# Four column tiles for the modulations that TensorE computes during the S5 scan

## The chip, the cores and the metric

The kernel runs on one core of a Trainium2 chip. The metric is the device time of one execution in microseconds; the kernel before takes 2045.85 us in the median of three runs (2044.94 to 2045.88).

## The reference

Two transformer-like blocks run one after the other on 256 tokens of width 1024, all in 32-bit floats. The first has attention and a mixture of 32 experts. The second has two layers, a retention layer and an S5 layer (a diagonal state-space scan), each followed by a convolutional feed-forward part. Every layer of the second block is modulated by a condition vector:

```
cond = silu(c)                                  # 1024 numbers
mod  = cond @ ada_w[i] + ada_b[i]               # 1024 x 6144 weights, for i = 0, 1
sh1, sc1, g1, sh2, sc2, g2 = split(mod, 6)
h = rms_norm(x) * (1 + sc1) + sh1
x = x + g1 * mixer(h)                           # retention for i = 0, S5 for i = 1
h = rms_norm(x) * (1 + sc2) + sh2
x = x + g2 * conv_ffn(h)
```

So there are twelve groups of 1024 modulations, each a product of one row of 1024 numbers with a 1024 x 1024 matrix (4 MB). The change concerns one of them, `sc2` of the S5 layer.

## The kernel before

A feature of the width-1024 vectors stands on a partition, so modulations are wanted as columns: 128 partitions by 8 columns for a group. Class `Columns` makes them. For eleven of the twelve groups `step` (L192) does it on VectorE: for each chunk `k` of 128 input features it multiplies the weights of that chunk (128 x 1024) by the chunk's condition number per partition and adds them up in `acc` (L201, L203), and `finish` (L208) sums over the partitions with eight matmuls against a column of ones (L214).

The group that `ADA_PE` names, number 10 (`sc2` of the S5 layer), is done by `part` (L220) on TensorE instead, during the scan. Its weights lie in memory as eight pieces of 128 x 1024: four for output features 0 to 511 and four for 512 to 1023, each with two chunks `k` of 512 columns. One call of `part` takes one piece and does two matmuls. The stationary operand is one column, `cond[:, k]`, and the moving one is 128 x 512 weights, so that the result is one row of 512 on one partition, added up over eight chunks in a bank of the accumulators (tile `s`). Behind every fourth call ScalarE copies the row out (L233), four transposes turn it into four columns (L236), and VectorE adds the bias (L239) and one (L241) into `mod`.

The pieces come through the stream `wa2`, a ring of two buffers of 128 x 1024 (`NADA2 = 2`). A load into a buffer is issued when the instruction that read the piece before last is done. These loads go through GpSimd's queue (POOL, L115), in order with the loads of the scan's own matrices (tiles `s5i` and `s5e`, L1779).

The scan has eight chunks `c`. `rotated_inputs(c)` makes its inputs with 16 matmul records (L1790), `scan(c)` runs on VectorE (L1801 to L1814), and `from_states(c)` gives the outputs with 8 records on L1825 and 16 on L1827. Chunks go in pairs to `gelu` (L1835 to L1840, ScalarE and VectorE in turn). `outputs` puts the result back in the order of tokens (L1757). Then come the gated products of the layer (`glu_half`, L251 to L253), which start behind `from_states(7)`. The loop calls `fill` twice for each chunk, and the table `FILL` says how many parts are to have been traced by then:

```
for c in range(8):
    if c < 7:
        rotated_inputs(c + 1)
    scan(c)
    fill(2 * c)
    ...
    last = from_states(c)
    fill(2 * c + 1)
```

The order on each engine is not that of the program: a planner with a cost model of its own goes through the program by priority and places an instruction where its engine is free by its reckoning. On the chip each engine then follows that fixed order, and an instruction that waits holds up all behind it. Behind the scan, `ada_step(4)` starts the next group on VectorE at low priority.

The same kernel uses column tiles at its start: `ada_tile` (L405) makes the first block's modulations with stationary operands of 32 columns (one or two of them in use, the rest zero) and puts the outputs of four matmuls on partitions 0 to 31, 32 to 63, 64 to 95 and 96 to 127 of one bank.

Of the kernel before, what the change touches and what calls it, by code (L numbers as in the profile page):

```python
# [8 lines left out]
F32 = mybir.dt.float32  # L9
# [20 lines left out]
ADA_PE = (10,)  # L30

ADA_F1 = (4, 7, 10, 13)
FILL = (0, 0, 0, 0, 1, 2, 3, 4, 5, 6, 7, 8, 8, 8, 8, 8, 8)
PREP_RET = 4
AHEAD = 2
LOW = 300
# [29 lines left out]
class Stream:  # L66
# [3 lines left out]
    def __init__(self, nc, pool, n, width, late=None):  # L70
        self.nc, self.pool, self.n, self.width, self.late = nc, pool, n, width, late
        self.sources, self.tiles, self.home = [], {}, {}
        self.issued = self.at = 0
        self.held = {}
# [109 lines left out]
class Columns:  # L184
# [2 lines left out]

    def __init__(self, g, cond, out, bias, scales):
        self.g, self.cond, self.out, self.bias, self.scales = g, cond, out, bias, scales
        self.n, self.u, self.pool, self.acc = 0, 3, None, None  # L190

    def step(self, bank=None):  # L192

# [25 lines left out]

    def part(self, bank, pool):  # L220

        g = self.g
        v = g.nc.vector
        u = self.u = (self.u + 1) % 4
        if u == 0:
            self.b = bank()
        w = g.wa.get()
        for k in range(2 * u, 2 * u + 2):
            g.nc.tensor.matmul(out=self.b[:1, :], lhsT=self.cond[:, k:k + 1], rhs=w[:, k % 2 * 512:(k % 2 + 1) * 512], start=(k == 0), stop=(k == 7))
        g.wa.issue(g.wa.at)  # L230
        if u == 3:
            row = pool.tile([1, 512], F32, tag="row", name="row")
            g.nc.scalar.copy(out=row, in_=self.b[:1, :])  # L233
            b = bank()
            for m in range(4):
                g.nc.tensor.transpose(out=b[:, m:m + 1], in_=row[:, m * 128:(m + 1) * 128], identity=g.ident[:1, :1])  # L236
            sl = slice(2 * self.n, 2 * self.n + 4)
            o = self.out[:, sl]
            v.tensor_tensor(out=o, in0=b[:, :4], in1=self.bias[:, sl], op=ALU.add)  # L239
            if self.n // 4 in self.scales:  # L240
                v.tensor_scalar(out=o, in0=o, scalar1=1.0, scalar2=None, op0=ALU.add)  # L241
            self.n += 2
# [1005 lines left out]
def sincos(nc, part, ang, n, out=None):  # L1248

    v, s = nc.vector, nc.scalar  # L1250
    k, r, m = part(n), part(n), part(n)
    v.tensor_scalar(out=k, in0=ang, scalar1=INV2PI, scalar2=MAGIC, op0=ALU.mult, op1=ALU.add)
    v.tensor_scalar(out=k, in0=k, scalar1=-MAGIC, scalar2=None, op0=ALU.add)
    v.scalar_tensor_tensor(out=r, in0=k, scalar=-TWOPI[0], in1=ang, op0=ALU.mult, op1=ALU.add)
    v.scalar_tensor_tensor(out=r, in0=k, scalar=-TWOPI[1], in1=r, op0=ALU.mult, op1=ALU.add)
    v.scalar_tensor_tensor(out=r, in0=k, scalar=-TWOPI[2], in1=r, op0=ALU.mult, op1=ALU.add)

    v.tensor_scalar(out=m, in0=r, scalar1=HALFPI, scalar2=-2 * HALFPI * 2, op0=ALU.is_gt, op1=ALU.mult)
    v.scalar_tensor_tensor(out=m, in0=r, scalar=HALFPI, in1=m, op0=ALU.add, op1=ALU.add)
    for t in (r, m):  # L1260
        v.tensor_scalar(out=t, in0=t, scalar1=PI_IN, scalar2=-PI_IN, op0=ALU.min, op1=ALU.max)
    c, sn = out or (part(n), part(n))
    s.activation(out=sn, in_=r, func=ACTF.Sin)
    s.activation(out=c, in_=m, func=ACTF.Sin)
    return c, sn
# [195 lines left out]
def second_block(tc, g, out):  # L1461
# [261 lines left out]
    with ExitStack() as e5:  # L1723
# [132 lines left out]
        def fill(i):  # L1856
            while at[0] < FILL[i]:
                ada.part(small_bank, p5)
                at[0] += 1
# [303 lines left out]
```

## Time and profile before

| what | value |
|---|---|
| median of 3 runs | 2045.85 us |
| the profiled execution: its time | 2045.55 us |
| the profiled execution: its span | 2043.9 us |
| TensorE matmul busy | 1943.4 us (95%) |
| VectorE busy | 1104.8 us (54%) |
| ScalarE busy | 649.2 us (32%) |
| GpSimd busy | 59.0 us (3%) |

The shares are means over the whole span. The stretch of the scan, 1700 to 1784 us, is a small part of it with limits of its own. A 32-bit matmul leaves two records in the trace, so a group of "x8" is four matmuls of the program. The time of an execution is 1.65 us longer than its span.

### The profile page before, as it was taken

What the parts mean: (1) busy time and instruction counts of PE and PEld (TensorE: products, weight loads), DVE (VectorE), ACT (ScalarE), POOL (GpSimd) and SP (SyncE); (2) the same over time, 40 slices, a digit from 0 to 9 for tenths busy, and PEclk for the clock granted to TensorE, in tenths of its full rate; (3) what the DMA queues carried; (4) which work ended last, traced back from release to release, by engine and by line L of the source; (5) the groups of instructions that cost most, each with busy time, mean ns of one, the idle gap of its engine ahead of it and who ended that gap; (6) DMA issues with size and microseconds to landing.
All of it is one profiled execution on the core that took longest, in us unless ns stands there. A gap on an engine that the chain in (4) does not pass through costs nothing. (4 is left out here: it accounts for less than half of the span.)

```text
span 2043.9 us, 29004 instructions
## 1 busy us (share of the span) xinstructions
PE 1943.4 (95%) x11188; PEld 1256.4 (61%) x11188; DVE 1104.8 (54%) x2360; ACT 649.2 (32%) x1134; POOL 59.0 (3%) x92
## 2 busy tenths in 40 slices
PE   6999989999999999999989999999999999999998
PEld 4756844333233333343333338888999998699998
DVE  3856654322222122132212238998898879779863
ACT  5455211000000000010000014445677645256542
POOL 1000010000000000000000000000011002100000
PEclk9999989999999999999999998999999999799999
DMA  8657659999999999999989994767677877555651
GB/s 342 223 197 282 240 193 413 427 426 427 426 427 427 426 427 427 426 421 387 427 366 427 426 394 159 259 235 267 228 258 260 288 279 295 206 193 195 226 178 63
DMA packets 101758, 643.41 MB, mean 315 GB/s; under 512 B 11584, under 2 KB 12880, under 8 KB 34288
## 3 DMA queue, kind: packets, MB, share of 16 engines
q1 hardware_dynamic: 94176, 613.46, 75.8%
q0 software_dynamic: 6624, 26.76, 3.8%
q8 instruction: 89, 1.46, 0.3%
q10 hardware_dynamic: 816, 1.30, 0.2%
q14 instruction: 53, 0.43, 0.1%
HBM read 626.79 MB, written 14.68 MB: 314 GB/s over the span
## 5 line engine op out<-in xcount | busy, mean ns | idle before, releaser
L956 PE MATMUL hc<-w,xe 128*64 128x512 f32 (+1 forms) x2008 | 470.3, 596 | 29.5 <-DMA w<-in_w_in_dram 28.3
L956 PEld LDWEIGHTS hc<-w,xe 128*64 128x64 f32 (+1 forms) x2008 | 145.4, 138 | 338.7 <-issue 244.0
L148 DVE TENSOR_TENSOR parts<-w,parts 128x1024 fp32r<-128x1024 f32 x238 | 289.8, 1222 | 64.2 <-ACT parts L147 60.0
L147 ACT CAST parts<-w 128x1024 fp32r<-128x1024 f32 x238 | 248.6, 1047 | 200.3 <-PE b L253 116.5
L251 PE MATMUL b<-h2h,parts 128*128 128x256 f32 x896 | 255.9, 286 | 1.4 <-ACT h2h L1527 0.9
L252 PE MATMUL b<-h2l,parts 128*128 128x256 f32 x896 | 255.5, 285 | 1.3 <-DVE h2l L1528 0.9
L956 PE MATMUL yb<-w,hb 128*64 128x512 f32 (+1 forms) x1024 | 252.5, 603 | 2.1 <-SPq L1205 1.6
L253 PE MATMUL b<-h2h,parts 128*128 128x256 f32 x896 | 254.3, 284 | 0.0
L976 DVE COPY hs<-hc 128x512 f32<-128x512 f32 x33 | 22.8, 691 | 405.3 <-PE hc L956 405.3
L251 PEld LDWEIGHTS b<-h2h,parts 128*128 128x128 f32 x896 | 170.1, 190 | 4.0 <-ACT h2h L1527 3.0
L252 PEld LDWEIGHTS b<-h2l,parts 128*128 128x128 f32 x896 | 169.9, 190 | 3.7 <-DVE h2l L1528 2.1
L253 PEld LDWEIGHTS b<-h2h,parts 128*128 128x128 f32 x896 | 169.8, 190 | 0.6 <-issue 0.6
L974 ACT COPY hs<-hc 128x512 f32<-128x512 f32 x33 | 19.3, 585 | 429.9 <-PE hc L956 429.9
L956 PEld LDWEIGHTS yb<-w,hb 128*64 128x64 f32 (+1 forms) x1024 | 68.1, 138 | 132.1 <-issue 120.9
L203 DVE SCALAR_TENSOR_TENSOR acc<-w,c,acc 128x1024 f32<-128x1024 f32 x77 | 98.5, 1279 | 7.3 <-DMA w<-in_ada_w_dram 7.0
L251 PE MATMUL b<-ah,parts 128*128 128x256 f32 x352 | 101.3, 288 | 0.7 <-ACT parts L147 0.6
L253 PE MATMUL b<-ah,parts 128*128 128x256 f32 x352 | 101.2, 287 | 0.0
L252 PE MATMUL b<-al,parts 128*128 128x256 f32 x352 | 100.5, 286 | 0.0
L938 PEld LDWEIGHTS gb<-S,h 128*128 128x128 f32 x544 | 68.2, 202 | 40.6 <-issue 30.9
L1019 ACT COPY ys<-yb 64x512 f32<-64x512 f32 (+1 forms) x32 | 18.5, 578 | 222.6 <-PE yb L956 222.5
L1562 PE MATMUL b<-parts,h2h 128*128 128x512 f32 x256 | 81.9, 400 | 1.4 <-DVE parts L148 0.8
L938 PE MATMUL gb<-S,h 128*128 128x128 f32 (+1 forms) x544 | 76.1, 293 | 6.2 <-issue 5.0
(521 smaller groups left out, 2967.0 us busy)
## 6 DMA issues: line engine op xcount, KB each, us to landing
w<-in_w_in_dram SPq DMA_DIRECT2D x252, 1024.0 KB, 19.4
w<-in_w_out_dram SPq DMA_DIRECT2D x128, 1024.0 KB, 19.5
w<-in_ffn_up_dram SPq DMA_DIRECT2D x44, 1024.0 KB, 4.9
w<-in_ada_w_dram SPq DMA_DIRECT2D x72, 512.0 KB, 5.1
w<-in_ret_w_in_dram SPq DMA_DIRECT2D x24, 1024.0 KB, 4.8
w<-in_ffn_down_dram SPq DMA_DIRECT2D x22, 1024.0 KB, 4.9
w<-in_w_ada_dram SPq DMA_DIRECT2D x32, 512.0 KB, 3.9
w<-in_ada_w_dram POOLq DMA_DIRECT2D x24, 512.0 KB, 4.8
```

Of the source, the lines that this page charges most:

```text
L147: self.nc.scalar.copy(out=hi, in_=w)
L148: self.nc.vector.tensor_tensor(out=lo, in0=w, in1=hi.bitcast(F32), op=ALU.subtract)
L203: v.scalar_tensor_tensor(out=self.acc, in0=w, scalar=cc, in1=self.acc, op0=ALU.mult, op1=ALU.add)
L251: pe.matmul(out=o, lhsT=w[0][:, sl], rhs=a[0][:, k], start=first, stop=False)
L252: pe.matmul(out=o, lhsT=w[0][:, sl], rhs=a[1][:, k], start=False, stop=False)
L253: pe.matmul(out=o, lhsT=w[1][:, sl], rhs=a[0][:, k], start=False, stop=last)
L938: g.got = pe.matmul(out=b[:, k * 128:k * 128 + n], lhsT=g.h2[:, t, d * 128:(d + 1) * 128], rhs=S[:, t, :n], start=(t == 0), stop=(t == 1))
L956: g.got = pe.matmul(out=on, lhsT=x, rhs=w[:, n * 512:n * 512 + 512], start=first, stop=last)
L974: s.copy(out=h, in_=hc[e][n])
L976: v.tensor_copy(out=h, in_=hc[e][n])
L1019: s.copy(out=o, in_=i)
L1562: pe.matmul(out=bs[t], lhsT=x[:, kk, tsl], rhs=y[:, k * 512:(k + 1) * 512], start=(kk == 0 and i == 0), stop=(kk == 7 and i == 2))
```

## The change

One call of `part` now takes two pieces (four chunks `k`) and does four matmuls. The condition is copied once into `padded`, 128 x 8 x 32, which GpSimd zeroes, so that each chunk has a stationary operand of 32 columns with the number in column 0. The four matmuls of a call write to the four column tiles of the bank (partitions 0, 32, 64 and 96 in use), and the second call adds to the first: two calls make 512 features where four calls did. ScalarE copies the whole bank, 128 x 512. In place of four transposes of one row, four matmuls against a column of ones both turn the row and sum it over the partitions. `FILL` counts to four calls instead of eight and puts them at every other place: behind `from_states` of chunks 2, 3, 4 and 5.

```
-FILL = (0, 0, 0, 0, 1, 2, 3, 4, 5, 6, 7, 8, 8, 8, 8, 8, 8)
+FILL = (0, 0, 0, 0, 0, 1, 1, 2, 2, 3, 3, 4, 4, 4, 4, 4, 4)
...
-        u = self.u = (self.u + 1) % 4
+        u = self.u = (self.u + 1) % 2
         if u == 0:
             self.b = bank()
-        w = g.wa.get()
-        for k in range(2 * u, 2 * u + 2):
-            g.nc.tensor.matmul(out=self.b[:1, :], lhsT=self.cond[:, k:k + 1], rhs=w[:, k % 2 * 512:(k % 2 + 1) * 512], start=(k == 0), stop=(k == 7))
+        if self.padded is None:
+            self.padded = pool.tile([128, 8, 32], F32, name="padded")
+            g.nc.gpsimd.memset(self.padded, 0.0)
+            v.tensor_copy(out=self.padded[:, :, 0], in_=self.cond)
+        ws = [g.wa.get() for _ in range(2)]
+        for k in range(4):
+            g.nc.tensor.matmul(out=self.b[32 * k:32 * k + 32, :], lhsT=self.padded[:, 4 * u + k], rhs=ws[k // 2][:, k % 2 * 512:(k % 2 + 1) * 512],
+                               start=(u == 0), stop=(u == 1))
         g.wa.issue(g.wa.at)
-        if u == 3:
-            row = pool.tile([1, 512], F32, tag="row", name="row")
-            g.nc.scalar.copy(out=row, in_=self.b[:1, :])
+        if u == 1:
+            row = pool.tile([128, 512], F32, tag="row", name="row")
+            g.nc.scalar.copy(out=row, in_=self.b)
             b = bank()
             for m in range(4):
-                g.nc.tensor.transpose(out=b[:, m:m + 1], in_=row[:, m * 128:(m + 1) * 128], identity=g.ident[:1, :1])
+                g.nc.tensor.matmul(out=b[:, m:m + 1], lhsT=row[:, m * 128:(m + 1) * 128], rhs=g.ones[:, :1], start=True, stop=True)
```

## Rows read from the trace of the kernel before

**Rows 1.** L229's records: nanoseconds min/median/max, first and last start, forms.
```profile
L229 PE MATMUL s<-w,c x32: 590/592/1057, 1701.0 to 1771.7; 128*1 128x512 f32 x32
```

**Rows 2.** Timeline: start, length, L405's and L229's groups on TensorE.
```profile
15.41 1.93 PE L405 MATMUL pm<-w,cz 128*32 128x512 f32 x8 [15.41 <-DVE rst L179]
...
19.95 1.07 PE L405 MATMUL pm<-w,cz 128*32 128x512 f32 x8
20.95 0.71 PE L412 MATMUL b<-dg,xr 128*128 128x128 f32 x4
...
31.80 2.78 PE L405 MATMUL pm<-w,cz 128*32 128x512 f32 x24
...
1700.98 1.02 PE L229 MATMUL s<-w,c 128*1 128x512 f32 x2
...
1741.66 3.57 PE L229 MATMUL s<-w,c 128*1 128x512 f32 x4
...
1748.10 1.88 PE L229 MATMUL s<-w,c 128*1 128x512 f32 x4
```

**Rows 3.** The chain that ended last, in order of time: start, length, what.
```profile
1741.73 3.50 PE s L229 x4
...
1747.05 0.45 PE c L1827 x4
...
1748.21 0.61 ACT g L1835
...
1769.22 3.50 PE s L229 x4
...
1773.79 0.35 PE s L236 x4
1774.16 0.16 DVE mod L239
```

**Rows 4.** Waits of 1700 to 1830: total, times, longest.
```profile
DVE g L1836 <- ACT g L1835: 10.5, 3, 5.7
...
DVE mod L239 <- PE s L236: 4.1, 1, 4.1
```

**Rows 5.** Stretches: length, busy us (instructions) by engine, granted clock, DMA.
```profile
1701.00:1705.50 4.50, 4.36 (x15) 1.28 (x14) 3.61 (x9) 4.39 (x10) 4.50 (x8) 1.00 0.87 270
...
1741.60:1745.20 3.60, 3.60 (x6) 0.38 (x5) 1.57 (x3) 0.28 (x1) 0.00 (x0) 0.50 0.96 368
...
1756.00:1760.00 4.00, 4.00 (x29) 3.06 (x28) 3.90 (x9) 2.58 (x6) 1.18 (x2) 1.00 0.35 94
1760.00:1763.00 3.00, 2.67 (x7) 0.42 (x6) 3.00 (x7) 0.21 (x1) 0.53 (x1) 1.00 0.91 332
1763.00:1766.00 3.00, 1.22 (x5) 0.36 (x3) 3.00 (x7) 0.63 (x1) 0.53 (x1) 1.00 0.66 213
1766.00:1769.10 3.10, 3.10 (x17) 3.03 (x16) 3.10 (x7) 0.00 (x0) 0.00 (x0) 0.56 0.43 160
...
1776.60:1781.30 4.70, 4.66 (x22) 4.66 (x23) 1.51 (x2) 0.00 (x0) 1.01 (x2) 0.50 0.57 184
```

**Rows 6.** POOL's timeline: the issue of loads for the ring.
```profile
1739.14 0.53 POOL L115 DMA_DIRECT2D w<-in_ada_w_dram  x1
...
1745.53 0.56 POOL L115 DMA_DIRECT2D w<-in_ada_w_dram  x1 [4.63 <-PE s L229]
```

**Rows 7.** Tile w, 1660 to 1830: its loads from issue to landing.
```profile
DMA to landing us min/median/max: 3.7/4.9/9.4
```

**Rows 8.** Groups nearest to the new instructions: row copy, sums, VectorE, memset.
```profile
L424 ACT COPY row<-pm x1: 586/586/586, 34.7 to 34.7; 128x512 f32<-128x512 f32 x1
...
L214 PE MATMUL yb<-ones,acc x16: 250/250/271, 286.6 to 288.3; 128*128 128x1 f32 x16
...
L239 DVE TENSOR_TENSOR mod<-s,pvt x2: 156/158/161, 1752.0 to 1774.2; 128x4 f32<-128x4 f32 x2
...
L1416 POOL MEMSET s5T<- 128x512 f32 x8 | 4.2, 524 | 925.5 <-PE yb L956 916.5 <-DMA s_scratch<-s5T 8.9
```

More of the change, by code (lines that the diff above doesn't have):

```diff
@@ L189, in __init__ @@
         self.g, self.cond, self.out, self.bias, self.scales = g, cond, out, bias, scales
-        self.n, self.u, self.pool, self.acc = 0, 3, None, None
+        self.n, self.u, self.pool, self.acc, self.padded = 0, 1, None, None, None
     def step(self, bank=None):
```

## The prediction

> **What bounds the kernel now.** I began with the page's shares: TensorE is busy 95% of the span, which would make every microsecond taken from it a gain. That is a mean, so I went to the stretch of the change, first to the line itself. L229 leaves 32 records, 590 ns each at the least and 1057 at the most, from 1701.0 to 1771.7 us [rows 1]. A record's length is not its price, because matmuls overlap. The timeline gives prices: four records (two matmuls) take 1.88 us from first start to last end at 1748.10 and 3.57 us at 1741.66 [rows 2]. So a record costs about 0.43 us in the first place ((1.88 - 0.59) / 3) and 0.87 us in the second; the windows show a granted clock of 0.50 there, the lower level of 1.2 GHz, against 1.00 or 2.4 GHz elsewhere [rows 5]. The median record is 592 ns long [rows 1], so most ran at the higher level; I count 24 there and 8, the two groups of the chain below, at the lower: 24 x 0.43 + 8 x 0.87 = 17.3 us of TensorE.
>
> Next came the chain that ended last, to see how much of that sets the end. Only two of the eight calls stand in it, both at the lower clock: 3.50 us from 1741.73 and 3.50 us from 1769.22 [rows 3]. The waits say whom they hold up [rows 4]. Behind the first stands the rest of `from_states`; then ScalarE's first step of gelu at 1748.21, and VectorE, which had a gelu instruction at its head, stood idle for 5.7 us. The second is the last call: behind it come the row copy, the transposes and L239 on VectorE at 1774.16, which stood in front of the last scan chunk for 4.1 us. The other six calls lie in time that TensorE had to spare: at 1701 to 1705.5 it waited for VectorE and ScalarE, and from 1760 to 1766 it was busy only 2.67 + 1.22 of 6 us while VectorE was busy all 6 [rows 5]. So the stretch is bound by VectorE with two stalls that TensorE causes; 17.3 us of work is worth at most those stalls.
>
> **The new calls.** The trace has the same construction at L405: 32-column stationary operands, outputs in four column tiles, 512 moving columns. Eight records (four matmuls) take 1.07 us at 19.95, and the next work starts 1.00 us after; three such sets take 2.78 us at 31.80; one takes 1.93 us at 15.41, where records last as long as L229's longest [rows 2]. Untiled, eight records would be 3.4 us at 0.43. So a call costs 1.0 us at the higher clock and 1.9 us at the lower, four calls 4.0 to 7.6 us, and 9.7 to 13.3 us leave TensorE.
>
> The Trainium skill, TensorEngine Tiling (Array Packing), Key Properties, speaks against this: changing the tiling mode drains TensorE, and each call changes it twice. By that rule alone a call in between full-array matmuls would cost visibly more than one among its like. Here it costs 1.00 us between L412's groups against 2.78 / 3 = 0.93 us among its like, so the drain is at most about 0.1 us a call, 0.4 us for four [rows 2], and the sum would move by that.
>
> **Stall one (1741.73).** A new call needs two pieces at once. The second of them is issued at 1739.14 [rows 6] and a landing takes 4.9 us in the median [rows 7], so it is there at about 1744.0 and the call can't stand where the old one stood unless it waits. Two cases bound it. If the call still runs in front of the rest of `from_states`, 3.50 becomes 1.9: a gain of 1.6. If it comes behind, the full 3.5 leaves, but the wide stream in which the clock came back leaves too, and the 22 of its 24 records that remain run at 0.212 us (4.66 / 22 at 0.50 [rows 5]) instead of the 2.9 us that they took: 4.7, so 3.5 - 1.8 = 1.7. Both give about the same; I take 1.7, with 3.5 as the upper end (the clock returns anyway) and 0 as the lower.
>
> **Stall two (1769.22).** Each pair of loads is released when a call ends: POOL issued 0.3 us after the release at 1745.23 [rows 3, 6]. Two issues of 0.53 and a landing of 4.9 make 6.3 us from a call's end to the next pair. With the second call ending near 1746 to 1747, the third can start near 1753 and end at 1754 to 1755, and the fourth near 1761 and end by 1763 or, pushed into the hole, by 1765.6. Old calls had to wait for a ring that gave one piece at a time: eight in a row, of which the last stood at 1769. The fourth new call thus fits the hole of 1763 to 1766, and with it the row and L239 are done before VectorE comes to them: the 4.1 us leave. If the call stays in place, it gives 3.50 - 1.9 = 1.6, less what the row costs more. The copy of 128x512 takes 586 ns, with as many elements on a partition as the old one, so nothing more; but eight records instead of four for the sums: L214's sixteen take 1.7 us from 286.6 to 288.3, so eight 0.85, some 0.5 more than the 0.35 that the four took on the chain [rows 3, 8]. So 1.1. I take 4.1, nearest to the row of the hole, and keep 1.1.
>
> **Small things.** The memset of 128x256 is half of L1416's 128x512 (524 ns), some 0.26 us; POOL has time for it ahead of the scan; without that cover it delays one load by 0.26. The copy of eight columns into `padded` costs as L239's 128x4, 0.16 us [rows 8], on a VectorE that is full early in the scan: 0.2. The first of the two rows lies beside VectorE work: 0. The loads of the next group start some 8 us earlier, so its VectorE work (L201, L203) can move ahead of or into the end of the scan; I take 0 and keep 1.3 us, one such instruction, both ways.
>
> **The sum.** 1.7 + 4.1 - 0.2 = 5.6 us from the profiled 2045.55: 2039.95. The median of the runs is 0.3 above that execution, so 2040.3. Behind the scan the products and the feed-forward part run on TensorE with loads far ahead, and I expect the 5.6 us to pass through to the end. Its own range is 2036 (3.5 + 4.1 + 1.3 + a little more) to 2042.
>
> **The rivals.** A change of 0.2%, 4.1 us, is about what a measurement of this kernel tells from none: faster means below 2041.8, slower above 2049.9.
>
> *The last call stays in place.* The fixed order keeps it behind the start of `from_states(6)`, or POOL holds the last pair behind scan loads. For it: POOL takes its loads in order and waits, 4.63 us for L229 ahead of the issue at 1745.53 [rows 6]. Against: those waits end sooner when calls do. Gain 1.7 + 1.1 - 0.2 = 2.6: 2043.3.
>
> *The clock.* The wide one-column matmuls also filled TensorE. After the stretch 1763 to 1766, in which it was busy 1.22 of 3 us, the clock fell to 0.56, and it came back behind 3.5 us of L229 [rows 5]. Without them it may stay at the lower level from 1746 on. In 1756 to 1766 TensorE is busy 7.89 us with 41 records; eight of L229 go (3.4), one call comes (1.9), and 33 narrow ones take 0.10 more each (0.212 against 0.112, four in 0.45 [rows 3]: 3.4): 9.8 of 10 us, so it becomes the bound there, and stall one's 1.7 is eaten. In 1701 to 1705.5 TensorE is busy 4.36 us, some 3 of them three groups of L229 like the one at 1700.98 [rows 2, 5]; with one call of 1.0 left it is half idle, and a fall as long as that of 1766 to 1769.1 at 0.56 would cost the stream behind it some 1.4 us [rows 5]. That leaves 5.6 - 1.7 - 1.4 = 2.5: 2043.4. The Trainium skill, TensorE: Matmul & The Clock Gate, Part 1, has the throttled level as the default that activity releases; the rows above agree in direction.
>
> *The ring (the other side).* Both buffers are read by one call, so no piece is in flight while a call runs, and each later call is 6.3 us behind the one before. TensorE's order is fixed: where the planner reckons the landing earlier than it is, the call waits at TensorE's head with `from_states` and `rotated_inputs` behind it, and VectorE waits for those. If three calls wait half of 6.3 each on the path, 9.5 us come and 5.6 go: 2049.8. It decides once calls are placed less than some 4 us behind the one before's end; five old calls stand in the 21 us from 1748.10 to 1769.22, some 5 apart [rows 2, 3], so such places are possible.
>
> *No overlap here.* That the tiles don't run together beside the scan, so that a call costs 3.4 us: L405 speaks against it in the same kernel. Then only the places change: about 2045.
>
> **How the numbers follow.** Forecast 0.42, last call in place 0.15, clock 0.22, ring 0.17, no overlap 0.04. Below 2041.8 lie most of the forecast (0.37), some of the clock and the last-call cases (0.09) and hardly any of the others: 0.47. Above 2049.9 lie half of the ring's and a little of a reordered stretch behind the scan: 0.14. Within: 0.39. The range goes from 2036 to 2048.5, which leaves out the upper part of the ring's cases and a few gains beyond both stalls.
>
> **What the next profile would show.** Four groups of x8 on the new matmul line, 1.0 us each at the higher clock and 1.9 at the lower; no chain piece of 3.5 us on that line; VectorE's wait at the head of gelu down from 5.7 to some 4 us, and its wait for the modulation's bias add gone. Wrong would be: a wait of that line for the ring's loads, narrow records at 0.21 us over most of 1746 to 1766, or TensorE idle with the scan's end no earlier than now.

## The result and the profile after

The change made the kernel slower: 2063.47 us in the median of twelve runs (2049.32 to 2075.50) against 2045.87 (2042.61 to 2056.97), a ratio of 1.0076, interval 1.0056 to 1.0096. That is about 15.5 us (0.0076 x 2045.9), where I had forecast 5.6 us less. A ratio leaves out a run more than 1.5% above the quickest of its kernel, which is one run of e4 below. The profiled execution of the kernel after took 2064.64 us, span 2062.9. Lines past the edit have moved by up to 6: L229 is now L234, L1790 L1796, L1827 L1833, L1835 and L1836 L1841 and L1842, L239 L245.

The scan is where the two profiles part. I measure it from the first instruction of L1801 (now L1807) on VectorE to the last matmul of `from_states(7)`. The windows give, for the kernel before and then the kernel after, stretch, length, busy us (instructions) of TensorE's matmuls and weight loads, VectorE, ScalarE and GpSimd, granted clock, DMA share and GB/s:

```profile
1711.00:1781.20 70.20, 64.72 (x388) 49.85 (x387) 56.33 (x114) 21.44 (x36) 14.38 (x25) 0.85 0.73 266
```

```profile
1718.20:1800.50 82.30, 78.46 (x390) 68.84 (x390) 56.37 (x113) 21.36 (x36) 14.23 (x25) 0.58 0.61 225
```

The scan is 12.1 us longer with the same work on VectorE (56.3 us), and TensorE is 13.7 us busier, though wide work had been taken from it. What differs most is the granted clock, 0.58 against 0.85. The same view of the kernel after, cut where the clock changes:

```profile
1724.00:1729.00 5.00, 3.43 (x31) 3.30 (x30) 4.87 (x13) 4.89 (x8) 1.24 (x2) 0.97 0.99 405
1729.00:1763.00 34.00, 34.00 (x160) 34.00 (x160) 20.54 (x41) 3.85 (x8) 6.41 (x11) 0.50 0.49 176
1763.00:1769.80 6.80, 6.74 (x42) 4.41 (x42) 4.30 (x11) 2.18 (x5) 2.32 (x4) 0.75 0.82 259
1769.80:1777.60 7.80, 7.80 (x38) 7.73 (x37) 7.66 (x18) 6.52 (x11) 0.56 (x1) 0.50 0.68 266
1777.60:1788.50 10.90, 8.70 (x22) 1.74 (x21) 8.97 (x17) 1.23 (x2) 1.59 (x3) 0.50 0.38 127
1788.50:1800.50 12.00, 12.00 (x57) 11.87 (x56) 4.24 (x9) 0.58 (x1) 1.59 (x3) 0.50 0.66 232
```

Read the second line first. For 34 us TensorE had a matmul in flight all the time, 160 narrow records (64 moving columns) of `rotated_inputs` and `from_states`, at 0.212 us each (34.00 / 160), and the clock stayed at 0.50, the lower level of 1.2 GHz. In that stretch VectorE is busy 20.54 us only: TensorE sets the pace. The level came back behind the eight records of the second call, at 1763.20, and went again at 1769.8. The kernel before has the same fall, from about 1735 on, but there four records of L229 stood at 1741.66 [rows 2], and from about 1746 the clock was at 1.00 again. The windows of the kernel before around [rows 5]'s 1741.60 to 1745.20:

```profile
1735.00:1738.00 3.00, 3.00 (x19) 3.00 (x18) 3.00 (x6) 0.40 (x1) 0.00 (x0) 0.61 0.93 359
1738.00:1741.60 3.60, 3.60 (x18) 3.54 (x17) 3.60 (x9) 0.12 (x1) 2.28 (x4) 0.50 0.48 142
...
1745.20:1748.10 2.90, 2.90 (x23) 2.83 (x23) 0.00 (x0) 0.00 (x0) 0.56 (x1) 0.88 0.76 268
1748.10:1752.00 3.90, 3.90 (x23) 2.22 (x22) 3.16 (x8) 2.27 (x4) 1.77 (x3) 1.00 0.72 248
```

The new line on TensorE's timeline of the kernel after, with two groups of `from_states` beside it (start, length, what, in brackets the idle time before it):

```profile
1708.46 1.06 PE L234 MATMUL s<-w,padded 128*32 128x512 f32 x6
...
1763.20 2.47 PE L234 MATMUL s<-w,padded 128*32 128x512 f32 x8
...
1777.65 1.92 PE L234 MATMUL s<-w,padded 128*32 128x512 f32 x4
1779.50 1.12 PE L1833 MATMUL c<-S,s5i 128*128 128x64 f32 x4
1780.55 1.92 PE L234 MATMUL s<-w,padded 128*32 128x512 f32 x4
1783.71 1.92 PE L234 MATMUL s<-w,padded 128*32 128x512 f32 x4 [1.24 <-DMA w<-in_ada_w_dram]
1786.60 1.92 PE L234 MATMUL s<-w,padded 128*32 128x512 f32 x4 [0.96 <-DMA w<-in_ada_w_dram]
1788.45 1.12 PE L1833 MATMUL c<-S,s5i 128*128 128x64 f32 x4
```

The third and fourth calls come in halves (two matmuls, x4): the third has the end of a `from_states` between its halves, and each half of the fourth waits for a piece of its own. A half costs at the lower level what I had put down for a whole, 1.92 us. The last three halves stand in front of `from_states(6)`, which begins at 1788.45. Its last input from VectorE was there at 1784.43, the end of this line of VectorE's timeline:

```profile
1784.02 0.41 DVE L1820 TENSOR_TENSOR S<-t,t 128x252 f32<-128x252 f32 x1
```

So ready work stood for some 4 us behind calls whose pieces came late, and the chain that ended last goes through their loads (start, length, what):

```profile
1765.44 6.80 DMA w<-in_ada_w_dram
...
1779.88 6.67 DMA w<-in_ada_w_dram x2
1786.55 0.04 issue
1786.60 1.92 PE s L234 x4
```

The waits from 1695 to 1805 (total us, times, longest):

```profile
ACT g L1841 <- PE c L1833: 36.7, 4, 11.8
...
DVE g L1842 <- ACT g L1841: 20.1, 4, 6.8
...
PEld s L234 <- DMA w<-in_ada_w_dram: 6.0, 3, 3.0
...
DVE mod L245 <- PE s L242: 5.0, 2, 3.5
...
PE s L234 <- DMA w<-in_ada_w_dram: 2.2, 2, 1.2
```

These answer to [rows 4]: the wait at gelu doubled (10.5 to 20.1), the wait for the bias add did not go (4.1 to 5.0), and the wait for the ring's loads, 1.6 us in the kernel before, is 6.0 + 2.2 = 8.2 us. So the profile offers two causes: a clock that stays low without the wide one-column work, and a ring whose pieces come too late. Both can be seen in it, so the profile alone does not choose.

Not all of the 19.0 us between the two spans is the scan's. In the profile of after the scan begins 7.2 us later, and 3.8 of these are there at 1640, where both kernels still have the same order of work; scans of kernels on either side began between 1709 and 1721. Behind the scan the two are equal, 262.7 us before and 262.4 after. So the size of the loss is taken from the runs, and the two profiles show where it can arise.

### The profile page after: what moved, and what is told of

Its sections match the earlier page's. It is cut to its first block, busy times and chain, and to the rows that moved or that the text cites. A ratio compares the mean times of both kernels' runs of the same rounds, so it can differ in the third digit from the quotient of the medians.

```text
span 2062.9 us, 29023 instructions
## 1 busy us (share of the span) xinstructions
PE 1960.0 (95%) x11196; PEld 1279.1 (62%) x11196; DVE 1105.3 (54%) x2361; ACT 648.8 (31%) x1134; POOL 59.0 (3%) x93
## 5 line engine op out<-in xcount | busy, mean ns | idle before, releaser
L148 DVE TENSOR_TENSOR parts<-w,parts 128x1024 fp32r<-128x1024 f32 x238 | 289.9, 1222 | 66.8 <-ACT parts L147 65.3
L203 DVE SCALAR_TENSOR_TENSOR acc<-w,c,acc 128x1024 f32<-128x1024 f32 x77 | 98.5, 1280 | 8.9 <-DMA w<-in_ada_w_dram 8.7
```

Source lines behind the costliest of these rows:

```text
L148: self.nc.vector.tensor_tensor(out=lo, in0=w, in1=hi.bitcast(F32), op=ALU.subtract)
L203: v.scalar_tensor_tensor(out=self.acc, in0=w, scalar=cc, in1=self.acc, op0=ALU.mult, op1=ALU.add)
```

## The experiments

Two theories. **The clock:** the wide one-column matmuls of L229 kept TensorE at the higher level; tiles take under a third of their time (1.07 us for eight records against 2 x 1.88 [rows 2]), so the level falls and the narrow matmuls around them cost twice as much. **The ring** (the rival): pieces in pairs land late, and the calls hold up TensorE's order. All ratios are to the kernel before on the same chip; e2 and e7 have six runs, the others eleven or twelve. The table gathers, from each run's own profile, the 512-column one-column records inside the scan, the granted clock and the length of the scan, and how long TensorE sat idle ahead of the modulation's line until one of its loads landed. Its last column is the ratio.

| run | one-column records | clock | scan us | idle for loads us | ratio (95%) |
|---|---|---|---|---|---|
| before | 26 | 0.85 | 70.2 | 1.6 | 1 |
| after | 0 | 0.58 | 82.3 | 8.2 | 1.0076 (1.0056 to 1.0096) |
| e1 one column, new places | 26 | 0.78 | 72.9 | 7.1 | 1.0009 (0.9991 to 1.0027) |
| e2 tiles, old places | 0 | 0.62 | 84.1 | 0 | 1.0100 (1.0067 to 1.0133) |
| e3 before, hardly any wide work | 2 | 0.57 | 82.4 | 0 | 1.0039 (1.0016 to 1.0062) |
| e4 change, six pieces not loaded | 0 | 0.64 | 77.3 | 0 | 1.0031 (1.0005 to 1.0058) |
| e7 change + 7 matmuls | 14 | 0.60 | 92.8 | 9.2 | 1.0105 (1.0067 to 1.0143) |
| e5 change + 14 | 28 | 0.86 | 74.5 | 12.3 | 1.0020 (0.9998 to 1.0042) |
| e9 as e4, + 14 | 28 | 0.85 | 70.6 | 0 | 1.0024 (1.0006 to 1.0042) |
| e10 as e2, + 14 | 28 | 0.86 | 75.2 | 0 | 1.0024 (1.0001 to 1.0046) |
| e12 change + 21 | 42 | 1.00 | 66.8 | 0 | 1.0004 (0.9989 to 1.0019) |
| e8 before + 7 | 40 | 0.99 | 62.8 | 0 | 0.9988 (0.9967 to 1.0008) |
| e13 the same again | 40 | 1.00 | 62.6 | 0 | 0.9984 (0.9970 to 0.9999) |
| e6 before + 14 | 54 | 1.00 | 66.4 | 0 | 0.9987 (0.9970 to 1.0004) |
| e11 before + 21 | 68 | 0.97 | 77.9 | 2.1 | 1.0016 (0.9991 to 1.0040) |

**The tiles undone, the places kept (e1).** Pairs of pieces and the new `FILL` stay; the matmuls are one column wide again, with the row and the transposes of before.

```
-            g.nc.tensor.matmul(out=self.b[32 * k:32 * k + 32, :], lhsT=self.padded[:, 4 * u + k], rhs=...,
-                               start=(u == 0), stop=(u == 1))
+            g.nc.tensor.matmul(out=self.b[:1, :], lhsT=self.cond[:, 4 * u + k:4 * u + k + 1], rhs=...,
+                               start=(u == 0 and k == 0), stop=(u == 1 and k == 3))
```

> Two pieces a call and the new places, but the old one-column matmuls, one row and transposes: everything of the change except the column tiles. Theory clock (the wide one-column matmuls were what held TensorE at its upper clock among the narrow ones of the scan; tiles take some 10 us of them away): near the kernel before, 2042 to 2050 us, narrow records mostly at 0.11 us. Theory ring (a call waits at TensorE's head for a pair of loads, with from_states behind it): as slow as the change, 2056 to 2066 us.

Measured: 2052.62 us against 2051.68, no difference shown. The modulation's line of this kernel, with its idle time:

```profile
L230 PE MATMUL s<-w,c x32: 590/592/1061, 1707.0 to 1780.2; 128*1 128x512 f32 x32
...
  DMA w<-in_ada_w_dram: 7.1, 4
```

TensorE waits for the ring's loads nearly as long as after the change, 7.1 against 8.2 us, and this costs nothing that can be measured. Its clock fell too, to 0.59 in the stretch from 1737, and came back behind eight wide records at 1755.47 (5.03 us).

**The tiles kept, the places undone (e2).** One piece a call in the eight old places; chunk `k` goes to tile `k % 4`, so that two tiles work at a time.

```
+        w = g.wa.get()
+        for k in range(2 * u, 2 * u + 2):
+            c = k % 4
+            g.nc.tensor.matmul(out=self.b[32 * c:32 * c + 32, :], lhsT=self.padded[:, k], rhs=w[...],
+                               start=(k < 4), stop=(k >= 4))
```

> Column tiles, but one piece a call, eight calls and the old places: chunk k goes to tile k mod 4, two matmuls side by side instead of four. Theory clock: slow like the change, 2054 to 2066 us, with most of the scan at the lower clock. Theory ring: the pair is gone, so 2038 to 2046 us.

Measured: 2071.23 us against 2051.68, slower by about as much as the change. No load is waited for: in the view of its modulation line nothing stands under the heading of idle time.

```profile
L235 PE MATMUL s<-w,padded x32: 592/1061/1062, 1707.0 to 1788.6; 128*32 128x512 f32 x32
...
its engine sat idle before it (us, times) until:
who waited for it (us, times):
```

With the windows of this run (eight of 5 us from 1737; first and last shown) the low level is seen to last:

```profile
1737.00:1742.00 5.00, 4.47 (x24) 4.37 (x23) 5.00 (x11) 1.23 (x2) 1.80 (x3) 0.60 0.92 325
...
1772.00:1777.00 5.00, 5.00 (x28) 4.88 (x31) 0.00 (x0) 0.44 (x1) 1.03 (x2) 0.50 0.68 212
```

e1 and e2 cut the change in two, and the loss goes with the tiles. The ring's waits go with the other half.

**Wide work taken out of the kernel before (e3).** Nothing of the change is in this kernel; all but the first chunk of each row of 512 cover only 64 of the features, so that most of the sums is left out.

```
+            n = 512 if k == 0 else 64
+            g.nc.tensor.matmul(out=self.b[:1, :n], lhsT=self.cond[:, k:k + 1], rhs=w[:, k % 2 * 512:k % 2 * 512 + n], ...)
```

> The kernel before, in which seven of the eight chunks of a product cover only the first 64 of 512 features (that part of the sum is left out): loads, ring, calls and places of the kernel before, but two wide matmuls instead of sixteen. Theory clock: slow although work is left out, 2054 to 2070 us. Theory ring, and my prediction's account that the calls only cost time on the chain: faster than before, 2036 to 2043 us.

Measured: 2060.95 us against 2051.68, slower by 0.16% at the least, with less work, the old ring and no new wait. The scan in the windows:

```profile
1716.90:1799.30 82.40, 74.15 (x384) 70.26 (x382) 56.45 (x114) 21.53 (x36) 14.27 (x25) 0.57 0.60 219
```

Length and clock are those of the kernel after. One of its twelve runs kept the clock (mean over the span 0.980, the others 0.963 to 0.970), and that one took 2040.37 us, where the others took 2056 to 2067.

**No loads behind the calls (e4).** The change, but calls 2 to 4 read the first call's two pieces again and the other six are not loaded, so that these modulations come from the wrong weights.

```
-        ws = [g.wa.get() for _ in range(2)]
+        if self.n % 4 == 0 and u == 0:
+            g.wa.issue(g.wa.at)
+            self.ws = [g.wa.tiles.pop(g.wa.at + i) for i in range(2)]
+            g.wa.at += 2
+        ws = self.ws
```

> The change, with calls 2 to 4 reading the two pieces of the first call (the other six pieces are neither loaded nor used): column tiles without the ring. Theory clock: still slow, 2052 to 2064 us. Theory ring: the waits are gone, 2034 to 2044 us.

Measured: 2059.61 us against 2051.68. Without any piece to wait for the kernel is still slower than before. Its interval only just meets that of the change (1.0058 and 1.0056), so the ring may have a share in the loss while the clock is low; this run does not settle it.

**Wide work put back beside the tiles (e5, e9), and added to the kernel before (e6).** Behind `from_states` of chunks 0 to 6 stand two more one-column matmuls of 512 columns each, into a bank that nobody reads: 14 matmuls, 28 records, 12 us of TensorE at the higher level (28 x 0.43).

```
+            if c < 7:
+                with tc.issue_after(last.ins):
+                    for _ in range(2):
+                        pe.matmul(out=warm[:1, :], lhsT=g.c2[:, :1], rhs=xT[:, :2].rearrange("p a t -> p (a t)"), start=True, stop=True)
```

> The change, and behind from_states of chunks 0 to 6 two wide one-column matmuls each (128x512, operands that lie in SBUF, a result that nobody reads): 14 more matmuls, some 12 us of TensorE at the upper clock. Theory clock: the extra work lifts the clock and the time falls from about 1.007 of the kernel before to 0.998 to 1.003 of it. Theory ring alone, or any account by TensorE's busy time: 1.007 to 1.013.

Measured: 2052.47 us against 2049.67. Work that is good for nothing took the ratio from 1.0076 to 1.0020, within the range of the clock theory, although TensorE sat idle for loads 12.3 us, more than without it. The scan of this kernel in the windows:

```profile
1718.70:1793.20 74.50, 69.28 (x419) 50.03 (x418) 56.44 (x113) 21.51 (x36) 14.22 (x25) 0.86 0.68 247
```

> The kernel before with the same 14 wide matmuls. Theory clock: its spells at the lower clock (10, 7 and 7 us in its profile) shrink, against 12 us more work on a TensorE with little room: 0.996 to 1.002 of the kernel before. An account by busy time: 1.003 to 1.006.

Measured: 2046.84 us against 2049.67; 12 us more work on an engine that the page calls 95% busy cost nothing that the runs show, and the scan of the profiled run was shorter (66.4 us at 1.00).

> e4 (calls 2 to 4 read the pieces of the first, six pieces are left out) with the 14 wide matmuls of e5. If clock and ring are all there is to the loss: 0.994 to 1.000 of the kernel before, below e4's 1.003. If e4's rest has another cause: 1.003 or more.

e9 is e4 with the same 14 matmuls. Measured: 2054.30 us against 2049.67, 1.0024, between the two ranges that I had expected: with the clock helped, taking the loads away gained nothing over e5 (1.0020).

**Half as much (e7, e8).** One matmul in each place in place of two.

> As e5 with one wide matmul behind each chunk instead of two. Theory clock: between the change and e5, 1.001 to 1.006 of the kernel before. Busy time: between the change and e5 on the other side, 1.007 to 1.010.

Measured: 2074.35 us against 2049.67, 1.0105, a miss. Half of the wide work did not bring half of the gain: the clock stayed at 0.60, the added records ran at the lower level and were in flight 13.0 us (14 records), and the scan took 92.8 us.

> The kernel before with one wide matmul behind each of seven chunks. Theory clock, as the runs so far have it (a dose that is too thin does not keep the level): the old wide work is there as well, so the clock of the scan comes to lie between the 0.85 of before and the 1.00 of the run with 14: 0.997 to 1.002 of the kernel before. Busy time: 1.001 to 1.004.

Measured: 2046.07 us against 2051.04, 0.9988. Its interval takes in 1, but in the profile the clock held: in the kernel before, whose own calls are wide, seven more brought the scan to 0.99.

**Single pieces and more (e10, e11).** e10 is e2 with the 14 matmuls; e11 is the kernel before with three in each place, 21.

> Column tiles with one piece a call at the old places (1.010 of the kernel before by itself) and the 14 wide matmuls. Theory clock with the ring of pairs as a second loss: the clock comes back to 0.85 or more and the ring is the old one, so 0.995 to 1.001, better than the change with the same wide work (1.002). If the ring of pairs costs nothing: 1.000 to 1.004.

Measured: 2054.93 us against 2051.04, 1.0024, in the range for a ring that costs nothing. With pairs (e5), with no loads (e9) and with single pieces (e10) the same 14 matmuls give 1.0020 to 1.0024 at clocks of 0.85 and 0.86: at these clocks a cost of the ring or of the places can't be told from none.

> The kernel before with 21 wide matmuls, three behind each of seven chunks. Clock theory: the scan was at 1.00 with 14 and TensorE busy 66.29 of 66.4 us, so more work only takes time, 6 us: 1.000 to 1.004. If the gain of 14 came from elsewhere: 0.996 to 1.000 again.

Measured: 2055.45 us against 2051.04, 1.0016: the gain of e6 is not seen, and a loss is not shown, since the interval takes in 1. The scan of the profiled run is 77.9 us, 11.5 longer than e6's, 6 of them the seven matmuls more (14 records x 0.43). The rest is not the added work alone: five of the next group's instructions (L203, 1.28 us each) lie in this scan and one in e6's, and about its last 4.5 us ran at the lower level.

**As much as brings the clock to 1.00 (e12), and e8 repeated (e13).**

> The change with 21 wide matmuls, three behind each of seven chunks: as much wide work in the scan as the kernel before with 14, since the tiles took about ten us of it away. If the clock is the whole loss, its scan runs at 0.95 or more and the time is 0.996 to 1.000 of the kernel before. If the change has another loss beside the clock (the ring of pairs, or the order that the planner made), it stays at 1.001 to 1.005 at the same clock.

Measured: 2051.03 us against 2050.69, 1.0004 (0.9989 to 1.0019): of the loss nothing can be seen any more, with some 18 us of work added (42 x 0.43). The value lies between the two ranges that I had expected, so a small second loss is not excluded. The scan in the windows, and the new line with its records at the higher level throughout:

```profile
1716.10:1782.90 66.80, 65.92 (x433) 45.92 (x432) 56.32 (x113) 21.65 (x36) 14.25 (x25) 1.00 0.74 265
```

```profile
L234 PE MATMUL s<-w,padded x32: 592/592/617, 1705.1 to 1774.1; 128*32 128x512 f32 x32
```

> The kernel of e8 (before, one wide matmul behind each of seven chunks) once more, since 0.9988 with an interval of [0.9967, 1.0008] told it from nothing. If the scan's clock is worth what its profile showed (62.8 us against 70.2): 0.996 to 0.999, and together with e8 clear of 1. If not: 0.999 to 1.002.

Measured: 2048.45 us against 2050.69, 0.9984 (0.9970 to 0.9999), in agreement with e8. The scan:

```profile
1716.40:1779.00 62.60, 61.26 (x401) 44.07 (x401) 55.26 (x113) 21.45 (x36) 13.92 (x24) 1.00 0.78 286
```

This is the best version that I ran: the kernel before with seven matmuls of no use, faster than both, though by little, some 3 us (0.0016 x 2050.69).

## Why the prediction was wrong

**The step that failed** is the price of the rival "the clock". I had the mechanism and its evidence, the fall of 1766 to 1769.1 that ended behind L229 [rows 5], but I counted it as something that eats 1.7 and 1.4 us of a gain, 3.1 us together, and left it out of the forecast's sum. That came from looking at two stretches of 10 and 4.5 us and taking the others as they were, "time that TensorE had to spare". TensorE had that spare time because it ran at 2.4 GHz, and the calls that I took away stood where they brought the level back. In the scan the records other than the modulation's took 49.05 us before (64.72 - 15.67, L229's 26 records) and 68.30 after (78.46 - 10.16, L234's 24): 19.2 us came with the lower clock, 5.5 went with the wide work, and 13.7 is what the windows show. That the 19.2 us go by the clock and not by the new order is seen at 1.00, where the same records took 40.3 us in the changed kernel (e12: 65.92 - 6.11 of L234 - 19.47 of the added ones) and 41.8 in the kernel before (e13: 61.26 - 12.29 - 7.14). My "9.8 of 10 us, so it becomes the bound there" was true of 34 us in a row.

That the clock carries the loss is shown from both sides: taken from the kernel before, the wide work makes a slower kernel at the clock of the changed one, 0.57 (e3, slower by half as much, with 15.67 - 4.84 = 10.8 us of work on this line left out), and put back into the changed one, it takes away most of the loss (e5) or all of it that can be seen (e12). In the table the clock follows the count of one-column records (0 to 14: 0.57 to 0.64; 26 to 28: 0.78 to 0.86; 40 and more: 0.97 to 1.00), with tiles or without, with loads or without.

The single runs say the same. At one mean clock over the span the changed kernel is not the slower one: its runs at 0.973, 0.974 and 0.977 took 2052.76, 2053.74 and 2049.32 us, while the kernel before, in the sets beside e1 to e13, took 2066.69 and 2056.76 us in its one run each at 0.973 and 0.974 and 2050.38 to 2056.36 in fourteen at 0.977. These sets are from other times and in part other chips, so this bounds any second loss only roughly. Most runs of the changed kernel lie lower, at 0.963 to 0.969.

The Trainium skill, TensorE: Matmul & The Clock Gate, Part 1, has the throttled level as the state from which activity releases TensorE. The trace agrees that the work decides, but it adds that a matmul in flight at every moment was no release here: 34.00 us busy of 34 at 0.50.

**The rival on the slower side, the ring,** gave 2049.8 us and a slower kernel, and its waits are there (8.2 us). They don't make the kernel slower by themselves, and it is slower without them: e1 has 7.1 us of them at 1.0009, e2 has none at 1.0100, e5 has 12.3 us at 1.0020. What hides them there I did not trace. A share of the ring while the clock is low stays open: in the profile of after the late calls hold `from_states(6)` up by some 4 us (the last call of the kernel before took 3.50 in its midst [rows 3]), and e4, without the loads, lies at 1.0031 against 1.0076, with intervals that just meet.

**The price of a call** held where a call ran in one piece: six of the first call's eight records took 1.06 us at 1708.46. It did not hold for calls in halves, since half a call costs as much as a whole: 1.05 us for x4 at the higher level (e12, at 1765.35), 1.92 at the lower (against 1.88 and 3.57 for two one-column matmuls [rows 2]). At a clock of 1.00 the 24 records in the scan were busy 6.11 us (e12) where 26 of one column were busy 12.29 (e13): some 6 us leave TensorE in the scan, not 9.7 to 13.3 (for all eight old calls, six of whose records stood ahead of it).

**Stall one and stall two** (1.7 and 4.1 us) did not leave, and their places were wrong. I put the second call near 1746 and the fourth into the hole of 1763 to 1766. The second stood at 1763.20, and the next pair of loads was issued behind it at 1765.44; the fourth ended at 1788.5, with the bias add waiting 3.5 us. I had expected VectorE's wait at gelu to fall to some 4 us; it had four, the longest 6.8. **The small things** were small: the memset (0.31 us at 1693.34) and the copy into `padded` lay ahead of the scan and beside other work. **No overlap** was rightly set aside.

Had the clock been held for nothing, the forecast might have been near, though no run shows it: the one run of e3 that kept it took 2040.37 us, and the quickest of e4, at a mean clock of 0.979, took 2039.31, both with work left out. With 21 matmuls (e12) the changed kernel's scan is 66.8 us at 1.00; the kernel before reaches 66.4 with 14 (e6). The 6 us that the tiles save are the seven matmuls more that it took to keep the level.

Two things stay open. One is why the level falls near 1730 to 1737 in most profiles, with small waits of TensorE ahead of it (3.43 us busy of 5 in the kernel after), and hardly in those with 40 and more one-column records. The other is why one kernel's runs differ so much. They go with the mean clock: the kernel after took 2049.32 us at 0.977 and 2075.50 at 0.963, and the 29 runs of before beside e11 went from 2039.53 us at 0.985 to 2066.69 at 0.973. So the level is no fixed property of a kernel; the change moved how often it is lost.

## What to carry to other kernels

Before work is taken from TensorE, look at the granted clock in the windows around it, and at what ran just before it rose: wide matmuls with a cheap stationary operand may be what holds the level for the narrow ones beside them, and then every narrow record's price is part of the sum, over the whole stretch and not only where the work stood. Where a change to TensorE moves the time the wrong way, add useless wide matmuls to both kernels: if the time falls and the granted clock of the stretch rises with it, the clock is a cause. Try more than one amount, since seven brought the changed kernel nothing here and fourteen did. A call that needs several loads has its full price advantage only if it runs in one piece; in halves it cost twice as much (2 x 1.05 us against 1.07), still less than the one-column matmuls (2 x 1.88).

## What the runs showed of the hardware

- TensorE can have a matmul in flight all the time and stay at 1.2 GHz: 34.00 of 34 us, 160 records of 64 columns with 128-column weight loads, granted clock 0.50.
- More work made the kernel faster: some 18 us of useless matmuls (21) brought the changed one from 1.0076 to 1.0004, six us (7) the kernel before to 0.9984 (0.9970 to 0.9999). Seven in the changed kernel (e7, 1.0105) were no better than none.
- Two tiles of four cost as much time as four: 1.05 us for four records (e12) against 1.07 for eight [rows 2].
